# Hybrid decoder step on one core: chunk 0 cast from raw x with the norm's weight as scale, matmuls of ones ahead, and the work ahead of chunk 2 put in another order

## The chip, the cores and the metric

One NeuronCore of a Trainium2 chip runs the whole step. The time is device time in microseconds, the median of several runs; the three runs of the kernel before gave 1186.17, 1187.00 and 1188.01 us. Engines are called as in the profile: PE is TensorE, DVE is VectorE, ACT is ScalarE, POOL is GpSimd, SP the queue that issues the DMAs.

## The reference

One layer on 2048 prompt tokens and 64 tokens of eight running sequences, 1024 wide:

```python
xn = rms_norm(x, norm_pre)                  # x * rsqrt(mean(x*x) + eps) * norm_pre
z  = xn @ w_in                              # 1024 -> 4096: v_pool, g_pool, u_lru, g_lru
y_pool = (windowed mean of v_pool - v_pool) @ pool_w * pool_scale     # windows 2, 4, 8, 16
xs = causal_conv(u_lru)                     # width 4
y_lru = scan(a(xs), u(xs))                  # gates: sigmoid(xs @ wa + ba), sigmoid(xs @ wx + bx)
out = concat(y_pool * silu(g_pool), y_lru * silu(g_lru)) @ w_out
y = x + rms_norm(out, norm_post)
```

Everything is float32. The kernel writes each operand of a large product as a rounded high part and a low part, and adds three products (high x high, high x low, low x high).

## The kernel before, in words

The 2112 tokens are cut into five chunks of 426 (the last has 408). `x` comes twice: transposed (`xt`, model channels on partitions, the moving operand of the products) and by token (`x`, 17 tiles of 128 tokens, called tok 0 to 16), from which the norm's factor r of each token is made.

How r is made: `tok_square` squares a token tile on ACT and sums it; `tok_rsqrt(i0, i1)` makes rsqrt for a range of tiles (DVE, two ACT steps, three DVE steps); `r_diag(c)` multiplies the identity by the factors of the tiles of chunk c (ACT, four or five pieces); `r_rows(c)` multiplies ones by that diagonal on PE, so that r of chunk c stands on all partitions in PSUM. The text calls these results r0 to r4. `normalise(c, r)` multiplies `xt` by r and the norm's weight (DVE, L272), casts the high part (ACT, L280) and subtracts for the low part (DVE or POOL, L289); it squares some token tiles between its casts.

Chunk 0 doesn't wait for its r: its x is multiplied by the norm's weight alone (`x_g` on DVE, `x_hi` on ACT, `x_lo` on DVE or POOL), and r0 is multiplied in after the product (`pool_evac` with `rs`, and L719 for the gates).

The first part of the program, up to L723, loads all this and does the blocks of pool group 0 for chunk 0: value blocks 0 and 1 (`v0_0`, `v1_0`) and gate blocks (`g0_0`, `g1_0`), each 8 steps of 3 matmuls (`z_k`). The loop at L728 does chunks 1 to 4 of the same group. For chunk 1 it does both value blocks, r2, one gate block, the pool map of chunk 0 (`pool_mm`, 12 matmuls) and the other gate block; normalising of chunk 2 goes on meanwhile. In chunk 2 comes value block 0, then r3, then value block 1. A pool map needs the windows of its chunk (`pool_window`, DVE L365 to L391, then a cast and a low part).

The order of work on each engine is the order of the code (the block stands under `tc.manual_schedule()`), and each engine takes its instructions one after the other. Loads go through the one SP queue in the order of the code; a load into a slot waits until the tile in it has been squared, and holds the loads behind it. Three slots hold three token tiles each; the slot of a tile is chosen by its number.

Of the kernel before, what the change touches and what calls it, by code (L numbers as in the profile page):

```python
# [55 lines left out]
R01_AT = 3  # L56
# [5 lines left out]
def hymba_kernel(  # L62
# [196 lines left out]
    def normalise(c, r, lo_engs, squares={}):  # L259
# [10 lines left out]
        for k in range(KT):  # L270
# [347 lines left out]
    with tc.manual_schedule():  # L618
        nc.sync.dma_start(out=parT, in_=par)
        load_x(0, 0, 1)  # L620
        stage_w(0, 0, 1)
        load_x(0, 1, 2)
        load_x(0, 2, 4)
        stage_w(1, 0, 1)
# [27 lines left out]
        x_g(2)
        x_hi(2)
        x_g(3)
        x_hi(3)
        x_lo(2, V)
        w_hi(0, 1, A)
        x_lo(3, G)
        w_lo(0, 1, V)
        x_g(4)  # L660
        x_hi(4)
        x_g(5)
        x_hi(5)
        x_lo(4, V)
        x_g(6)
        x_hi(6)
        x_lo(5, G)
# [2 lines left out]
        x_g(7)  # L670
        x_hi(7)
        x_lo(6, V)
        x_lo(7, V)
# [3 lines left out]
        for i in range(3):  # L677
# [811 lines left out]
```

## Time and profile before

| | |
|---|---|
| median of three runs | 1187.0 us (1186.17 to 1188.01) |
| the profiled execution | 1190.4 us, of which the span from first to last instruction 1188.4 us |
| PE busy | 1167.1 us, 98% |
| DVE, ACT, POOL busy | 828.8 us (70%), 552.4 us (46%), 356.9 us (30%) |
| granted TensorE clock, mean | 0.997 |

Times in the rows are from the span's start. A matmul's row starts when it starts; its length holds the way out of the array, so that the distance of two starts, not the length, is what one costs. In a row of the timeline the brackets at the end give the idle time of that engine just before it, and what ended it.

### The profile page before, as it was taken

What the parts mean: (1) busy time and instruction counts of PE and PEld (TensorE: products, weight loads), DVE (VectorE), ACT (ScalarE), POOL (GpSimd) and SP (SyncE); (2) the same over time, 40 slices, a digit from 0 to 9 for tenths busy, and PEclk for the clock granted to TensorE, in tenths of its full rate; (3) what the DMA queues carried; (4) which work ended last, traced back from release to release, by engine and by line L of the source; (5) the groups of instructions that cost most, each with busy time, mean ns of one, the idle gap of its engine ahead of it and who ended that gap; (6) DMA issues with size and microseconds to landing.
All of it is one profiled execution on the core that took longest, in us unless ns stands there. A gap on an engine that the chain in (4) does not pass through costs nothing.

```text
span 1188.4 us, 16263 instructions
## 1 busy us (share of the span) xinstructions
PE 1167.1 (98%) x5794; PEld 1076.0 (91%) x5794; DVE 828.8 (70%) x1201; ACT 552.4 (46%) x1015; POOL 356.9 (30%) x486
## 2 busy tenths in 40 slices
PE   7999999999999999999999999999999999999997
PEld 6899999999999999999999999999878878888886
DVE  4787334443625557888888888889877668888787
ACT  5753311211231236767676776767745233345232
POOL 4145402410431243333333433334310002221332
PEclk9999999999999999999999999999999999999999
DMA  9712533532630210111111111104479766767553
GB/s 344 264 59 65 188 132 111 183 115 79 199 94 30 67 49 26 45 44 40 38 40 53 49 45 45 40 34 120 134 217 286 212 188 202 220 204 231 151 168 133
DMA packets 127905, 146.94 MB, mean 124 GB/s; under 512 B 12432, under 2 KB 87440, under 8 KB 127824
## 3 DMA queue, kind: packets, MB, share of 16 engines
q1 hardware_dynamic: 127824, 145.91, 39.3%
q8 instruction: 45, 0.74, 0.3%
q14 instruction: 36, 0.29, 0.1%
HBM read 106.37 MB, written 39.24 MB: 123 GB/s over the span
## 4 chain that ended last, share of the span: by engine, by line
PE 84%; DVE 5%; DMA 5%; ACT 3%; issue 2%; POOL 1%; SPq 0%; DVEq 0%; ACTq 0%; POOLq 0%
PE p L979 7%; PE p L978 7%; PE p L977 7%; PE v L302 5%; PE v L304 5%; PE v L303 5%; PE u L302 5%; PE u L304 5%; PE u L303 5%; PE g L302 5%; PE lg L302 5%; PE lg L304 5%; PE lg L303 5%; PE g L303 5%; PE g L304 5%
## 5 line engine op out<-in xcount | busy, mean ns | idle before, releaser
L504 DVE SCALAR_TENSOR_TENSOR xs<-u,parT,xs 128x426 f32<-128x426 f32 (+1 forms) x120 | 109.2, 910 | 46.7 <-ACT xs L500 30.5
L302 PE MATMUL v<-xh,w 128*128 128x426 f32 (+2 forms) x320 | 116.9, 365 | 7.1 <-ACT w L595 6.0
L303 PE MATMUL v<-xl,w 128*128 128x426 f32 (+2 forms) x320 | 116.1, 363 | 0.9 <-DVE xl L611 0.6
L970 POOL TENSOR_TENSOR xr<-ac,xr 128x512 f32<-128x512 f32 x28 | 47.7, 1723 | 229.7 <-DVE ac L1108 125.5
L302 PE MATMUL g<-xh,w 128*128 128x426 f32 (+1 forms) x320 | 114.6, 358 | 0.0
L304 PE MATMUL v<-xh,w 128*128 128x426 f32 (+2 forms) x320 | 114.1, 362 | 0.4 <-DVE w L109 0.4
L304 PE MATMUL g<-xh,w 128*128 128x426 f32 (+1 forms) x320 | 113.9, 356 | 0.2 <-POOL w L109 0.2
L303 PE MATMUL g<-xl,w 128*128 128x426 f32 (+1 forms) x320 | 113.8, 356 | 0.0
L302 PE MATMUL u<-xh,w 128*128 128x426 f32 (+1 forms) x320 | 113.7, 355 | 0.0
L302 PE MATMUL lg<-xh,w 128*128 128x426 f32 (+1 forms) x320 | 113.7, 355 | 0.0
L304 PE MATMUL lg<-xh,w 128*128 128x426 f32 (+1 forms) x320 | 113.5, 355 | 0.0
L304 PE MATMUL u<-xh,w 128*128 128x426 f32 (+1 forms) x320 | 113.4, 354 | 0.0
L303 PE MATMUL lg<-xl,w 128*128 128x426 f32 (+1 forms) x320 | 113.4, 354 | 0.0
L303 PE MATMUL u<-xl,w 128*128 128x426 f32 (+1 forms) x320 | 113.3, 354 | 0.0
L1270 DVE RECIPROCAL rv<-rv 128x426 f32<-128x426 f32 (+1 forms) x40 | 112.4, 2811 | 0.0
L977 PE MATMUL p<-ws,s 128*128 128x512 f32 (+1 forms) x264 | 102.4, 388 | 0.0
L978 PE MATMUL p<-ws,s 128*128 128x512 f32 (+1 forms) x264 | 102.0, 386 | 0.2 <-DVE ws L109 0.2
L979 PE MATMUL p<-ws,s 128*128 128x512 f32 (+1 forms) x264 | 102.0, 386 | 0.1
L979 PE MATMUL p<-ws,a 128*128 128x512 f32 x192 | 75.8, 395 | 1.1 <-DVE a L109 1.1
L978 PE MATMUL p<-ws,a 128*128 128x512 f32 x192 | 75.8, 395 | 1.1 <-DVE ws L109 1.1
L977 PE MATMUL p<-ws,a 128*128 128x512 f32 x192 | 75.8, 395 | 0.3 <-ACT ws L106 0.3
L365 DVE TENSOR_TENSOR s<-e 128x440 f32<-128x440 f32 (+3 forms) x40 | 28.8, 720 | 64.2 <-ACT e L336 48.5
(225 smaller groups left out, 2805.5 us busy)
## 6 DMA issues: line engine op xcount, KB each, us to landing
a<-mixed SPq DMA_DIRECT2D x112, 256.0 KB, 4.3
wr<-in_w_in SPq DMA_DIRECT2D x56, 256.0 KB, 3.1
tok<-in_x SPq DMA_DIRECT2D x16, 512.0 KB, 10.2
wo<-in_w_out SPq DMA_DIRECT2D x32, 256.0 KB, 3.8
wtd<-wo SPq DMA_DIRECT2D x32, 256.0 KB, 2.4
w<-wtd SPq DMA_DIRECT2D x32, 256.0 KB, 3.8
xr<-in_x SPq DMA_DIRECT2D x32, 256.0 KB, 3.8
out<-xr SPq DMA_DIRECT2D x30, 256.0 KB, 2.6
```

The lines of the kernel that those rows point to most:

```text
L302: nc.tensor.matmul(out, lhsT=wh, rhs=xh, start=(k == 0), stop=False)
L303: nc.tensor.matmul(out, lhsT=wh, rhs=xl, start=False, stop=False)
L304: nc.tensor.matmul(out, lhsT=wl, rhs=xh, start=False, stop=(k == KT - 1))
L365: nc.vector.tensor_tensor(out=dst[:, first:L], in0=src[:, first:L], in1=src[:, first - sh:L - sh], op=ALU.add)
L504: nc.vector.scalar_tensor_tensor(out=xs, in0=E[:, k:k + n], scalar=col(C_CW + 8 * k, b), in1=xs, op0=ALU.mult, op1=ALU.add)
L970: (eng or nc.vector).tensor_tensor(out=out, in0=a, in1=b, op=op)
L977: nc.tensor.matmul(out, lhsT=ah, rhs=wh, start=start and k == 0, stop=False)
L978: nc.tensor.matmul(out, lhsT=ah, rhs=wl, start=False, stop=False)
L979: nc.tensor.matmul(out, lhsT=al, rhs=wh, start=False, stop=stop and k == KT - 1)
L1270: nc.vector.reciprocal(out=v, in_=v)
```

## The change

It touches the part ahead of chunk 2 alone.

- Chunk 0: `x_g` goes. ACT casts the high part from raw x with the norm's weight as scale, and DVE makes every low part from raw x, the weight and the high part in one instruction. DVE casts the weights' high parts of both value blocks.
- PE: eight matmuls of a 128x128 tile of ones with itself ahead of the first value matmul, and two more behind each of the first three steps. Value block 1 runs two steps behind block 0 instead of four.
- Loads: the parameters come third; tok 3 to 6, which chunk 1's r needs, ahead of tok 0 to 2; tok 9 ahead of chunk 3's x; chunk 1's x in four pieces.
- r1 alone is made in gate block 1 of chunk 0, two steps later than before; r0 moves into chunk 1's first gate block, and with it the evictions of chunk 0 (`first_evac`) and squares 8 and 9; r2 moves into chunk 1's second gate block. Both gate blocks now stand ahead of chunk 0's pool map.
- Squares: tok 0, 1, 2, 7 between the casts of chunk 1; 10, 11, 12 between those of chunk 2, each followed by the load of tok 13, 14, 15 into its slot; 13 to 16 behind them.

```diff
-R01_AT = 3
+R1_AT = 5
+R0_AT = 2
+R2_AT = 4
+N_WARM = 8
+N_FILL = 2
@@ normalise
                 nc.scalar.copy(out=xn[c][0][:, p], in_=src)
+                lo()
+                los.append((p, src))
                 for j in squares.get(k, ()):
                     tok_square(j)
-                lo()
-                los.append((p, src))
+                    if j in reload:
+                        load_tok(reload[j], slots[2], j % 3)
...
     def x_hi(k):
-        A.copy(out=xn[0][0][:, k * CW:(k + 1) * CW], in_=xg[k])
-
-    def x_lo(k, eng):
+        A.activation(out=xn[0][0][:, k * CW:(k + 1) * CW], in_=x_part(0, k), func=AF.Copy, scale=col(C_NP, k))
+
+    def x_lo(k):
         p = slice(k * CW, (k + 1) * CW)
-        eng.tensor_tensor(out=xn[0][1][:, p], in0=xg[k], in1=xn[0][0][:, p].bitcast(F32), op=ALU.subtract)
+        V.scalar_tensor_tensor(out=xn[0][1][:, p], in0=x_part(0, k), scalar=col(C_NP, k),
+                               in1=xn[0][0][:, p].bitcast(F32), op0=ALU.mult, op1=ALU.subtract)
...
-        nc.sync.dma_start(out=parT, in_=par)
         load_x(0, 0, 1)
         stage_w(0, 0, 1)
+        nc.sync.dma_start(out=parT, in_=par)
...
-        for i in range(3):
-            load_tok(i, slots[0])
+        for i in range(3, 7):
+            load_tok(i, slots[i // 6 * 2], i % 3)
         for h in range(2):
             nc.sync.dma_start(out=w9r[h], in_=w_in[9, :, 512 * h:512 * (h + 1)])
...
+        for k in range(0, KT, 2):
+            load_x(1, k, k + 2)
+        for i in range(3):
+            load_tok(i, slots[1], i)
+        for i in range(7, 9):
+            load_tok(i, slots[2], i % 3)
...
+        warm = s_psum("warm")[:, :P]
+
+        def ones_mm(n):
+            for _ in range(n):
+                nc.tensor.matmul(warm, lhsT=ones, rhs=ones, start=True, stop=True)
+
+        ones_mm(N_WARM)
...
-        lag = 4
+        lag = 2
         for k in range(KT + lag):
             if k < KT:
                 z_k(Z0[0], wt[0], 0, k)
+            if k < lag + 1:
+                ones_mm(N_FILL)
             if k >= lag:
                 z_k(Z0[1], wt[1], 0, k - lag)
...
         r_diag(1)
-        r_diag(0)
-        for k in range(KT):
-            if k == R01_AT:
-                r1, R0 = r_rows(1), r_rows(0)
-                A.copy(out=r0, in_=R0)
-            z_k(Z0[3], wt[9], 0, k)
-        normalise(1, r1, [V], {3: (7,), 5: (8,), 7: (9,)})
...
+        for k in range(KT):
+            if k == R1_AT:
+                r1 = r_rows(1)
+            z_k(Z0[3], wt[9], 0, k)
+        normalise(1, r1, [V], {1: (0,), 3: (1,), 5: (2,), 7: (7,)})
+        tok_rsqrt(0, 3)
+        r_diag(0)
         pw0 = split_small(pw0r, 512, "pw0")
...
+        def first_evac():
+            R0 = r_rows(0)
+            A.copy(out=r0, in_=R0)
+            for j in range(2):
+                E, prevE0[j] = pool_evac(j, j, 0, Z0[j], None, r0)
+                Es.append(E)
+            for j in range(2):
+                V.tensor_tensor(out=sgs0[j], in0=Z0[2 + j], in1=r0, op=ALU.mult)
...
             if c == 1:
                 for k in range(KT):
                     for j in range(2):
                         z_k(Z[j], wt[j], c, k)
-                r = r_rows(n)
+                Zg = [gate(0, R0_AT, first_evac, s_psum)]
                 for j in range(2):
                     evac(j)
-                Zg = [gate(0)]
+                for i in range(8, 10):
+                    tok_square(i)
+                tok_rsqrt(7, 10)
+                r_diag(2)
+                for i in range(10, 13):
+                    load_tok(i, slots[2], i % 3)
+                for j in range(2):
+                    ds0.append(pool_window(j, 0, 0, Es[j]))
+                r2 = []
+                Zg.append(gate(1, R2_AT, lambda: r2.append(r_rows(2))))
+                r = r2[0]
...
             if c == 1:
-                for i in range(15, 17):
-                    load_tok(i, slots[2])
+                for i in range(13, 17):
                     tok_square(i)
+                    if i == 13:
+                        load_tok(16, slots[2], 1)
                 tok_rsqrt(10, 17)
                 r_diag(3)
                 silus()
```

How the order moves. PE, gate block 1 of chunk 0 before: `r_305` is r1 and `r_310` is r0, `g_0_115` the gate block.

```order
L304 MATMUL g_0_115<-xh_106,w_0_104 128x426
L255 MATMUL r_305<-dg_286,ones 128x86
L255 MATMUL r_305<-dg_286,ones 128x128 x2
L255 MATMUL r_305<-dg_286,ones 128x84
L255 MATMUL r_310<-dg_291,ones 128x128 x3
L255 MATMUL r_310<-dg_291,ones 128x42
L302 MATMUL g_0_115<-xh_106,w_0_104 128x426
```

PE in chunk 1's first gate block (`g_1_406`) of the kernel after: `r_413` is r0.

```order
L308 MATMUL g_1_406<-xh_316,w_0_102 128x426
L309 MATMUL g_1_406<-xl_317,w_0_102 128x426
L310 MATMUL g_1_406<-xh_316,w_0_102 128x426
L259 MATMUL r_413<-dg_346,ones 128x128 x3
L259 MATMUL r_413<-dg_346,ones 128x42
```

r0 has moved behind the whole of chunk 1's value blocks.

ACT from the copy of r0 to the diagonal of r2 (`dg_370`) before; the squares are the rows that write `tok` from `tok`.

```order
L703 COPY r_111<-r_310 128x426
L280 CAST xh_331<-xr_136 128x426 x2
L280 CAST xh_331<-xr_136 128x852
L224 ACTIVATE tok_110,tok<-tok_110 128x1024
...
L224 ACTIVATE tok_109,tok<-tok_109 128x1024
L230 ACTIVATE tok<-tok 128x3
L231 ACTIVATE tok<-tok 128x3
L248 ACTIVATE dg_370<-ident,tok 128x44
```

The same stretch after, where `dg_468` is the diagonal of r2 and `e_1` are the evictions of chunk 1's value blocks.

```order
L706 COPY r_111<-r_413 128x426
L342 COPY e_1_450<-v_1_356 128x426
L342 COPY e_1_455<-v_1_357 128x426
L228 ACTIVATE tok_110,tok<-tok_110 128x1024 x2
L234 ACTIVATE tok<-tok 128x3
L235 ACTIVATE tok<-tok 128x3
L252 ACTIVATE dg_468<-ident,tok 128x44
```

The copy of r0 stood ahead of the casts of chunk 1; it now stands behind them, and squares 8 and 9 stand behind it.

ACT from the third square inside chunk 2's casts to the diagonal of r3 before (`dg_545`):

```order
L224 ACTIVATE tok_110,tok<-tok_110 128x1024
L280 CAST xh_514<-xr_144 128x852
L224 ACTIVATE tok_110,tok<-tok_110 128x1024
L224 ACTIVATE tok_110,tok<-tok_110 64x1024
L230 ACTIVATE tok<-tok 128x7
L231 ACTIVATE tok<-tok 128x7
L248 ACTIVATE dg_545<-ident,tok 128x2
```

and after (`dg_578`):

```order
L228 ACTIVATE tok_110,tok<-tok_110 128x1024
L284 CAST xh_543<-xr_148 128x852
L228 ACTIVATE tok_110,tok<-tok_110 128x1024 x3
L228 ACTIVATE tok_110,tok<-tok_110 64x1024
L234 ACTIVATE tok<-tok 128x7
L235 ACTIVATE tok<-tok 128x7
L252 ACTIVATE dg_578<-ident,tok 128x2
```

Two squares stood between the last cast and the rsqrt; now four do.

## Rows read from the trace of the kernel before

**Rows 1.** The page's first part: busy time of each engine, share of the span, instructions.

```profile
PE 1167.1 (98%) x5794; PEld 1076.0 (91%) x5794; DVE 828.8 (70%) x1201; ACT 552.4 (46%) x1015; POOL 356.9 (30%) x486
```

**Rows 2.** Busy time by stage: the stage, its length, busy time of PE, PEld, DVE, ACT and POOL with instructions, granted TensorE clock, DMA share and GB/s.

```profile
0.00:60.50 60.50, 51.32 (x228) 45.81 (x229) 36.33 (x67) 40.97 (x81) 17.90 (x41) 0.97 0.81 299
60.50:140.00 79.50, 79.50 (x440) 77.68 (x440) 49.84 (x98) 32.62 (x64) 36.77 (x41) 1.00 0.30 93
```

**Rows 3.** Timeline of PE, chunk 0: start, length, engine, line, operation, tiles, form, count, idle time before and what ended it.

```profile
5.99 0.72 PE L302 MATMUL v<-xh,w 128*128 128x426 f32 x1 [5.99 <-ACT w L595]
...
11.18 0.72 PE L303 MATMUL v<-xl,w 128*128 128x426 f32 x1 [0.58 <-DVE xl L611]
...
13.75 0.72 PE L302 MATMUL v<-xh,w 128*128 128x426 f32 x1 [0.40 <-ACT xh L607]
...
19.52 0.40 PE L302 MATMUL v<-xh,w 128*128 128x426 f32 x1
...
23.65 0.36 PE L302 MATMUL g<-xh,w 128*128 128x426 f32 x1
```

**Rows 4.** Timeline of PE around r1 with r0 (30.06), the end of chunk 1's value blocks (44.06), r2 (45.60), the start of chunk 2 (60.53) and r3 (65.20).

```profile
30.06 1.87 PE L255 MATMUL r<-dg,ones 128*128 128x86 f32 x16
31.76 0.44 PE L302 MATMUL g<-xh,w 128*128 128x426 f32 x1
...
44.06 0.35 PE L304 MATMUL v<-xh,w 128*128 128x426 f32 x1
45.60 0.42 PE L255 MATMUL r<-dg,ones 128*128 128x44 f32 x2 [1.19 <-ACT dg L248]
46.40 1.38 PE L255 MATMUL r<-dg,ones 128*128 128x128 f32 x6 [0.38 <-ACT dg L248]
...
60.53 0.36 PE L302 MATMUL v<-xh,w 128*128 128x426 f32 x1
...
65.20 1.20 PE L255 MATMUL r<-dg,ones 128*128 128x2 f32 x10
66.24 0.44 PE L302 MATMUL v<-xh,w 128*128 128x426 f32 x1
```

**Rows 5.** Busy time of the stretch behind r2's wait, columns as in rows 2.

```profile
46.90:50.30 3.40, 3.40 (x12) 3.24 (x12) 2.92 (x10) 3.40 (x8) 0.71 (x1) 0.50 0.16 63
```

**Rows 6.** Timeline of ACT in chunk 2's normalising: the third square (tok 14), the last square's accumulator read (tok 16), and four pieces of r3's diagonal.

```profile
55.94 1.06 ACT L224 ACTIVATE tok<-tok 128x1024 f32<-128x1024 f32 x1
...
60.03 0.19 ACT L224 ACTIVATION_READ_ACCUMULATOR tok<-tok 64x1 f32 x1
...
61.54 1.21 ACT L248 ACTIVATE dg<-ident,tok 128x128 f32<-128x128 f32 x4 [0.45 <-DVE tok L234]
```

**Rows 7.** DMA issues in five narrow stretches: tiles, queue, operation, count, KB each, us from issue to landing. In order: issued at 1.72, at 5.35 (the last piece of chunk 0's x), at 26.98 (tok 9), at 53.34 (tok 15) and at 55.19 (tok 16).

```profile
wst<-in_w_in SPq DMA_DIRECT2D x1, 256.0 KB, 3.2
...
xr<-in_xt SPq DMA_DIRECT2D x1, 426.0 KB, 6.8
...
tok<-in_x SPq DMA_DIRECT2D x1, 512.0 KB, 16.5
...
tok<-in_x SPq DMA_DIRECT2D x1, 512.0 KB, 3.7
...
tok<-in_x SPq DMA_DIRECT2D x1, 256.0 KB, 3.6
```

**Rows 8.** Timelines of DVE and POOL in chunk 0: low part of the first weight, the last two low parts of x on DVE, and what POOL did then.

```profile
5.97 0.69 DVE L598 TENSOR_TENSOR w<-wst,w 128x512 fp32r<-128x512 f32 x1
...
16.01 3.28 DVE L611 TENSOR_TENSOR xl<-x0g,xh 128x426 fp32r<-128x426 f32 x2
...
15.81 4.64 POOL L598 TENSOR_TENSOR w<-wst,w 128x512 fp32r<-128x512 f32 x3 [0.65 <-DVE w L595]
```

**Rows 9.** Timeline of ACT: diagonals of r1 and r0, copy of r0, accumulator read of tok 9's square and the last three pieces of r2's diagonal, evictions of chunk 1's value blocks.

```profile
28.69 2.31 ACT L248 ACTIVATE dg<-ident,tok 128x86 f32<-128x86 f32 x8 [0.70 <-DVE tok L234]
...
31.97 0.52 ACT L703 COPY r<-r 128x426 f32<-128x426 f32 x1 [0.97 <-PE r L255]
...
43.49 1.06 ACT L224 ACTIVATE tok<-tok 128x1024 f32<-128x1024 f32 x1 [3.27 <-DMA tok<-in_x]
44.46 0.19 ACT L224 ACTIVATION_READ_ACCUMULATOR tok<-tok 128x1 f32 x1
...
45.94 0.98 ACT L248 ACTIVATE dg<-ident,tok 128x128 f32<-128x128 f32 x3 [0.40 <-DVE tok L234]
...
50.32 0.91 ACT L336 COPY e<-v 128x426 f32<-128x426 f32 x2
```

**Rows 10.** Timeline of DVE, normalising of chunk 1: first products, first and last low part.

```profile
31.12 1.23 DVE L272 SCALAR_TENSOR_TENSOR xr<-xr,parT,r 128x426 f32<-128x426 f32 x2 [2.52 <-PE r L255]
32.97 0.61 DVE L289 TENSOR_TENSOR xl<-xr,xh 128x426 fp32r<-128x426 f32 x1 [0.62 <-ACT xh L280]
...
40.26 1.04 DVE L289 TENSOR_TENSOR xl<-xr,xh 128x852 fp32r<-128x852 f32 x1 [0.80 <-ACT xh L280]
```

**Rows 11.** Timeline of DVE: last step of the rsqrt for r2, first step of chunk 0's windows, first products and last two low parts of chunk 2.

```profile
45.75 0.16 DVE L234 SCALAR_TENSOR_TENSOR tok<-tok 128x3 f32<-128x3 f32 x1
...
46.84 0.59 DVE L365 TENSOR_TENSOR s<-e 128x426 f32<-128x426 f32 x1
...
50.10 2.37 DVE L272 SCALAR_TENSOR_TENSOR xr<-xr,parT,r 128x426 f32<-128x426 f32 x4 [0.34 <-issue]
...
57.11 2.10 DVE L289 TENSOR_TENSOR xl<-xr,xh 128x852 fp32r<-128x852 f32 x2
```

More of the change, by code (lines that the diff above doesn't have):

```diff
@@ L215, in hymba_kernel, with load_tok @@
     tok_box = {}
-    def load_tok(i, slot):
+    def load_tok(i, slot, pos):
         lo, hi = i * P, min((i + 1) * P, T_ALL)
-        t = tok_box[i] = slot[:hi - lo, i % 3 * D:(i % 3 + 1) * D]
+        t = tok_box[i] = slot[:hi - lo, pos * D:(pos + 1) * D]
         nc.sync.dma_start(out=t, in_=x[lo:hi, :])
@@ L257, in r_rows, with normalise @@
         return R
-    def normalise(c, r, lo_engs, squares={}):
+    def normalise(c, r, lo_engs, squares={}, reload={}):
         W = XR[c][1] - XR[c][0]
@@ L618, in hymba_kernel @@
     with tc.manual_schedule():
-        nc.sync.dma_start(out=parT, in_=par)
         load_x(0, 0, 1)
         stage_w(0, 0, 1)
+        nc.sync.dma_start(out=parT, in_=par)
         load_x(0, 1, 2)
+        stage_w(1, 0, 1)
         load_x(0, 2, 4)
-        stage_w(1, 0, 1)
         stage_w(0, 1, 2)
@@ L641, in hymba_kernel @@
         load_x(2, 0, 8)
-        x_g(0)
+        warm = s_psum("warm")[:, :P]
[3 more added lines that the diff above has]
+        ones_mm(N_WARM)
         x_hi(0)
-        w_hi(0, 0, A)
-        x_lo(0, V)
+        w_hi(0, 0, V)
+        x_lo(0)
         w_lo(0, 0, V)
-        x_g(1)
         x_hi(1)
-        x_lo(1, G)
+        x_lo(1)
         w_hi(1, 0, V)
         w_lo(1, 0, G)
[L652 to L658, printed above, removed]
-        w_lo(0, 1, V)
[L660 to L667, printed above, removed]
+        for k in range(2, 4):
+            x_hi(k)
+            x_lo(k)
+        w_hi(0, 1, V)
+        w_lo(0, 1, V)
+        for k in range(4, 6):
+            x_hi(k)
+            x_lo(k)
         w_hi(1, 1, V)
         w_lo(1, 1, G)
[L670 to L673, printed above, removed]
+        for k in range(6, 8):
+            x_hi(k)
+            x_lo(k)
         for h in range(2):
@@ L676, in hymba_kernel @@
             w_lo(8, h, G)
-        for i in range(3):
+        for i in range(3, 7):
             tok_square(i)
@@ L681, in hymba_kernel @@
             w_lo(9, h, G)
-        for i in range(3, 7):
-            tok_square(i)
-        for i in range(7, 9):
-            load_tok(i, slots[2])
+        load_tok(9, slots[2], 0)
         load_x(3, 0, KT)
-        lag = 4
+        lag = 2
         for k in range(KT + lag):
@@ L690, in hymba_kernel @@
                 z_k(Z0[0], wt[0], 0, k)
+            if k < lag + 1:
+                ones_mm(N_FILL)
             if k >= lag:
                 z_k(Z0[1], wt[1], 0, k - lag)
-        for i in range(9, 12):
-            load_tok(i, slots[1])
-        tok_rsqrt(0, 7)
+        tok_rsqrt(3, 7)
         for k in range(KT):
@@ L735, in evac, with gate @@
                 E[j], prev[j] = pool_evac(j, j, c, Z[j], prev[j], None)
-            def gate(j):
-                Zg = z_psum(f"g{j}_{c}")[:, :W]
+            def gate(j, at=None, then=None, ps_tile=z_psum):
+                Zg = ps_tile(f"g{j}_{c}")[:, :W]
                 for k in range(KT):
+                    if k == at:
+                        then()
                     z_k(Zg, wt[8 + j], c, k)
@@ L771, in hymba_kernel @@
             if n:
-                last = normalise(n, r, LO_ENGS[n], {1: (12,), 3: (13,), 5: (14,)} if c == 1 else {})
+                last = normalise(n, r, LO_ENGS[n], {1: (10,), 3: (11,), 5: (12,)} if c == 1 else {},
+                                 {i: i + 3 for i in range(10, 13)})
             if c == 1:
-                for i in range(15, 17):
-                    load_tok(i, slots[2])
+                for i in range(13, 17):
                     tok_square(i)
+                    if i == 13:
+                        load_tok(16, slots[2], 1)
                 tok_rsqrt(10, 17)
@@ L786, in hymba_kernel @@
                 hr = [fold_load(1, 0)]
-            Zg.append(gate(1))
+            if c > 1:
+                Zg.append(gate(1))
             todo_silu = Zg
```

26 lines of the change are left out of this document (1 added, 25 removed).

## The prediction, made before the changed kernel was run

> **What bounds the kernel now.** I read the page first, then the busy time by stage, then the timelines of the first 66 us. TensorE is busy 98% of the span [rows 1]. The stages show where the rest lies: of the first 60.5 us it works 51.3, and from 60.5 to 140 it works all 79.5 at full clock [rows 2]. So a microsecond gained or lost ahead of chunk 2 is carried to the end, and the change touches that part alone. TensorE's long waits there are two: 5.99 us for the first operands [rows 3], and 1.19 + 0.38 us for the scales of chunk 2, r2 [rows 4].
>
> The timeline shows one more loss. Value matmuls of 426 columns stand about 0.355 us apart until 19.52 and 0.195 us after it, though the engine waits no more from 13.75 on [rows 3]; 426 columns at 1.2 GHz are 0.355 us. The profile's clock column does not show that phase, the spacing does. The wait for r2 is followed by the same thing: after those 1.57 us the granted clock is 0.50 for 3.4 us [rows 5], which costs 1.7 us.
>
> The place that decides is r3, the scales of chunk 3: a few small matmuls that TensorE reaches at 65.20 [rows 4]. ScalarE has finished their operand at 61.54 + 1.21 = 62.75 [rows 6]. That chain (squares of the token tiles, rsqrt, diagonal) is only 2.45 us ahead of TensorE. If TensorE comes earlier and the chain does not, the gain ends there.
>
> **The change, step by step.** The sum follows both chains from the start to r3; times are from the span's start.
>
> *Start.* The parameters are now the third issue. The piece issued in that place, at 1.72, took 3.2 us [rows 7]: 4.9. The cast (0.55 us) no longer waits for a VectorE product: first value matmul about 5.5 instead of 5.99. A cast that scales by a column has no row of this size; bounds are the plain 0.55 and some 0.2 more, as the diagonals (128 columns, 0.32 apart, with such a scale) cost about that above a plain cast [rows 9]. I take 0.55; only the first of the eight is on the path. The new low part, one instruction of two inputs, is like the products of chunk 1, 0.6 us [rows 10], what the subtraction alone took.
>
> *Clock and value blocks.* After its last start wait at about 6.8 (VectorE makes the low parts of x and of the weight one after the other, 0.6 and 0.7 us [rows 8]) the filler keeps TensorE going. Before, 5.8 us without a wait went ahead of the fast spacing (13.75 to 19.52); I take the same: 12.6. One ones matmul is 128 of the 852 fp32 columns that took 1.70 us (30.06 to 31.76 [rows 4]), 0.26 us at full and 0.5 at half clock, so the six fillers take 3.0 us of the 7.1 between 5.5 and 12.6, waits 1.0, and about 9 of 48 matmuls the rest. 39 x 0.195 = 7.6: the value blocks end at 20.2, not 23.65 [rows 3]. Supply does not hold them: the last x lands at 5.35 + 6.8 = 12.15 [rows 7], its casts end about 13.2, and two low parts at the 1.6 us each that VectorE showed beside GpSimd [rows 8] give 16.5. Moving the low parts from GpSimd to VectorE costs nothing while that is so; should the clock be fast from the start, they are the bound (rival 1).
>
> *r1.* 39 more matmuls (gate block 0, five steps of gate block 1), 7.6 us: 27.8 (30.06 before). Its diagonal started at 28.69 behind seven squares [rows 9]; four are left, three of 1.04 us less, and its four pieces take 1.2: 26.8 at the latest. No wait. r1 is half of the 1.70 us: 28.65; VectorE starts at 28.85.
>
> *Chunk 1 normalised.* Before: 31.12 to 41.3, 10.2 us, with waits of 0.62 us behind the copy of r0 and 0.80 behind a late token tile [rows 10]. Both go: 8.8, end 37.65. TensorE reaches chunk 1 at 30.4, only 9 matmuls behind r1 where it had 15, and now waits for the low parts: about 0.3, 0.4 and 1.0 us (ready 1.85, 3.5 and 5.7 us after VectorE's start, wanted at 30.4, 32.0 and 33.5). 48 matmuls and 1.7: end 41.5, before 44.26 [rows 4].
>
> *r0 and r2.* Tile 9, now issued ahead of chunk 3's x about 24 us (once tile 6 is squared), has landed by 41 even at its old 16.5 us [rows 7], and square 9 wants it at 46. Two steps (1.2) and r0 (0.85): 43.5. ScalarE's queue now holds, behind that: copy of r0 0.5, two evictions 0.9, squares 8 and 9 at 1.06 [rows 9]: 47.2. From a square's end to the last piece of a diagonal it was 44.65 to 46.92, 2.3 [rows 9]: 49.5. TensorE does 30 matmuls and is there at 49.3. So the r2 stall goes, 1.57 us and 1.7 of clock. r2, 12 matmuls, the pool map's 12: chunk 2 could start at 55.0, where it was 60.53 [rows 4]. TensorE has gained 5.5 us here.
>
> *VectorE and ScalarE have not.* VectorE's rsqrt ends 1.25 after the square (44.65 to 45.9 [rows 11]): 48.45. The windows of chunk 0, until now done while TensorE was elsewhere, come here: 2.9 us (46.84 to 50.10 less 0.34 idle). Chunk 2's normalising starts at 51.3, before 50.10 [rows 11]: 1.2 us later. It takes 9.1 (to 59.2), so to 60.4, and TensorE, which eats a step of one block in 0.6 us, is held by it and reaches r3 at 61.0, 4.2 earlier than before.
>
> *Squares.* Before, tiles 12, 13, 14 were squared inside this stage and 15, 16 behind it. Now it is 10, 11, 12, and four are left. The reloads of 13, 14 and 15 wait for the slots of 10, 11 and 12. The third square of the stage ended 6.95 us after its start (55.94 + 1.06 [rows 6] against 50.10): 58.3. Then tile 15 is loaded into that slot, 3.7 us on an idle queue [rows 7]: 62.0. Squares 15 and 16, 2.3: 64.3 (16's own load, 3.6 us [rows 7], started earlier, behind square 13). On SP the reloads hold back only the stores of chunk 0's pool map, which come after r3. From the end of the last square to the last piece of the diagonal it was 60.2 to 62.75, 2.55 [rows 6]: 66.9, before 62.75. So 4.15 later, against a slack of 2.45.
>
> On the load the Trainium skill, DMA: Bandwidth & Descriptors, section "Anatomy of one DMA", gives 2.0 us fixed and the bytes at 436 GB/s for another path: 3.2 us for 512 KB, by my estimate. By it the sum below would be 0.5 smaller; the row's 3.7 decides.
>
> *At r3.* TensorE idles from 61.0 to about 65.2 (first, 2-column piece) and 0.8 more; r3 ends 0.3 behind the last piece, 67.2 against 66.24: +1.0. 5 us of idleness is three times what went ahead of the halved clock at r2, so I add that price once, +1.7; bounds are 0 (it stays) and 3.4 (two such stretches). What follows is bound by TensorE as before.
>
> Sum: +1.0 + 1.7 = +2.7 us. The profiled execution took 1190.4 with a span of 1188.4; it would be 1193.1. The median of the runs is 1187.0, 3.4 below it; +2.7 on that is **1189.7 us**.
>
> **Rivals.**
> 1. *The clock is free sooner.* If the ones matmuls alone bring the fast spacing before the first value matmul, the value blocks are bound by the low parts: 16.5, less what is then done, about 17.9 instead of 20.2. All steps up to the diagonal of r3 follow from r1, so 2.3 us come off: +1.0 - 2.3 + 1.7 = +0.4, 1187.4. For it: the ones are there from the start, so the eight can run through the 5 us in which TensorE idled. Against it: no row shows what matmuls of constants do to the clock, and those of 11 to 13.7 us, with gaps of 0.4 to 0.6 us between them, did not raise it [rows 3]. The Trainium skill, TensorE: Matmul & The Clock Gate, Part 1, "What's actually happening", says that the low clock is the resting state, that activity releases it, and that the moment is not tied to a kernel's start; by it this rival would come true in some executions and not in others.
> 2. *The 1187.0 holds no r2 stall.* The profiled execution is 3.4 us above the median, and its r2 stall is 1.57 + 1.7 = 3.3 us; tile 9 landed 16.5 us after its issue [rows 7], in a full queue. If it lands sooner in unprofiled runs, there is nothing left to save at r2, and the chain to r3, which no full queue holds, stays where it is: +2.7 + 3.3 = +6.0, 1193.0. Against it: some of the 3.4 may be the profiler's.
> 3. *The r3 wait does not come* (not slower). If reloads and squares hide so that the diagonal is there at 62.75 as before, TensorE waits 1.7 us instead of 5: r3 ends at 63.1, -3.1, and with the clock kept 1183.9. It decides from a diagonal at about 63.5 on. For it: ScalarE is idle between squares while reloads are under way. Against it: each load, square and rsqrt in the chain has a row, and their order is fixed.
>
> **How the numbers follow.** Forecast (r3 wait of 4 to 5 us, clock price once) 0.42, on its own 1188.0 to 1191.4; rival 1 0.26; rival 2 0.18; rival 3 0.14. A change below 0.2% (2.4 us) can't be told from none. Slower: rival 2 and about three quarters of the forecast, 0.50. Same: the rest of the forecast and rival 1, 0.37. Faster: rival 3, 0.13. The range goes from inside rival 3 and the lower half of rival 1 (1186.2) to rival 2 (1193.2).
>
> **What would show it.** First value matmul 5.3 to 5.7; fast spacing from about 12.6 (before 8: rival 1); r1 near 28; r2 without a wait; chunk 2's first matmul near 55; then TensorE waiting 4 to 5 us for ScalarE's diagonal at r3, with four squares behind chunk 2's last cast, and a clock of 0.50 behind it. No r3 wait, or a diagonal before 63.5, would make the forecast wrong, and so would a place later than chunk 2 that gives back or takes more than 1 us.

## The result, and the profile after

The changed kernel took 1191.65 us, the median of 7 runs (1190.91 to 1195.05), beside 1188.01 for the kernel before on the same chip; the ratio is 1.0038, 95% interval 1.0026 to 1.0051. On 1187.5 us, about the median of the kernel before in the later comparisons, the ratio is +4.5 us (3.1 to 6.1). The ratio is formed from all runs; the two medians alone differ by 3.6 us. The forecast was +2.7 us, below that interval.

The profiled execution took 1190.91 us with a span of 1189.0. The page's first part answers to [rows 1]; TensorE is as busy as before.

```profile
PE 1168.5 (98%) x5822; PEld 1079.1 (91%) x5822; DVE 829.3 (70%) x1202; ACT 552.9 (47%) x1015; POOL 355.0 (30%) x483
```

The busy time by stage, columns as in [rows 2]: the first 60.5 us, then two short stretches in which the granted clock is 0.50 (level 1.2 GHz), then up to 140.

```profile
0.00:60.50 60.50, 54.18 (x270) 49.40 (x270) 33.90 (x66) 36.95 (x73) 14.39 (x38) 0.97 0.78 282
12.20:15.60 3.40, 3.40 (x11) 3.19 (x10) 3.40 (x6) 2.74 (x5) 1.43 (x1) 0.50 1.03 420
...
66.80:73.60 6.80, 5.58 (x19) 5.30 (x20) 4.14 (x10) 5.71 (x15) 1.41 (x2) 0.50 0.12 44
73.60:140.00 66.40, 66.40 (x362) 64.87 (x362) 45.50 (x87) 25.56 (x48) 34.83 (x39) 1.00 0.29 84
```

Of the first 60.5 us TensorE is now busy 54.18 (51.32 in [rows 2]), the ones matmuls included. From 66.8 to 73.6 it works 5.58 of 6.8 us, and at half clock. The timeline of TensorE says why; it answers to [rows 3] and [rows 4]: the ones matmuls, the first value matmul, the wait for step 2, gate block 0 (21.08), r1, r0, r2, the start of chunk 2 (56.51), r3 in two parts and the second value block (70.34).

```profile
1.12 3.79 PE L648 MATMUL warm<-ones 128*128 128x128 f32 x16 [1.12 <-DVE ones L122]
5.67 0.46 PE L308 MATMUL v<-xh,w 128*128 128x426 f32 x1 [0.77 <-ACT xh L607]
...
10.33 0.46 PE L308 MATMUL v<-xh,w 128*128 128x426 f32 x1 [1.42 <-ACT xh L607]
...
21.08 0.35 PE L308 MATMUL g<-xh,w 128*128 128x426 f32 x1
...
28.63 1.01 PE L259 MATMUL r<-dg,ones 128*128 128x86 f32 x8
...
43.50 0.98 PE L259 MATMUL r<-dg,ones 128*128 128x128 f32 x8
...
50.23 1.05 PE L259 MATMUL r<-dg,ones 128*128 128x44 f32 x8
...
56.51 0.35 PE L308 MATMUL v<-xh,w 128*128 128x426 f32 x1
...
67.76 0.59 PE L259 MATMUL r<-dg,ones 128*128 128x2 f32 x2 [4.80 <-ACT dg L252]
68.61 1.93 PE L259 MATMUL r<-dg,ones 128*128 128x128 f32 x8 [0.27 <-ACT dg L252]
70.34 0.70 PE L308 MATMUL v<-xh,w 128*128 128x426 f32 x1
```

r1, r0 and r2 wait for nothing (their rows have no brackets). Chunk 2 starts 4.0 us sooner than in [rows 4]. Then TensorE stands still for 4.80 + 0.27 us at r3, and the second value block, at 66.24 before, starts at 70.34.

What r3 waits for is on ScalarE: the squares of tiles 13 to 16 behind the casts of chunk 2, and the diagonal.

```profile
60.49 1.06 ACT L228 ACTIVATE tok<-tok 128x1024 f32<-128x1024 f32 x1
...
62.34 1.06 ACT L228 ACTIVATE tok<-tok 128x1024 f32<-128x1024 f32 x1 [0.70 <-DMA tok<-in_x]
...
63.66 1.06 ACT L228 ACTIVATE tok<-tok 128x1024 f32<-128x1024 f32 x1 [0.17 <-DMA tok<-in_x]
...
65.69 1.06 ACT L228 ACTIVATE tok<-tok 64x1024 f32<-64x1024 f32 x1 [0.88 <-DMA tok<-in_x]
...
68.16 1.21 ACT L252 ACTIVATE dg<-ident,tok 128x128 f32<-128x128 f32 x4 [0.45 <-DVE tok L238]
```

Three of the four wait for their reload. The last, tile 16, is issued behind square 13 (60.49 + about 1.0); the list of DMA issues between 61 and 62 gives it 3.9 us, so it lands near 65.4, and its square starts at 65.69:

```profile
tok<-in_x SPq DMA_DIRECT2D x1, 256.0 KB, 3.9
```

### The profile page after: what moved, and what is told of

It reads as the page before. It is cut to its first block, busy times and chain, and to the rows that moved or that the text cites. A ratio compares the mean times of both kernels' runs of the same rounds, so it can differ in the third digit from the quotient of the medians.

```text
span 1189.0 us, 16330 instructions
## 1 busy us (share of the span) xinstructions
PE 1168.5 (98%) x5822; PEld 1079.1 (91%) x5822; DVE 829.3 (70%) x1202; ACT 552.9 (47%) x1015; POOL 355.0 (30%) x483
## 4 chain that ended last, share of the span: by engine, by line
PE 79%; DMA 7%; DVE 7%; ACT 4%; issue 2%; POOL 1%; SPq 0%; DVEq 0%; ACTq 0%; POOLq 0%
PE p L983 6%; PE p L984 6%; PE p L982 6%; PE v L309 5%; PE v L308 5%; PE v L310 5%; PE u L308 5%; PE u L310 5%; PE u L309 5%; PE lg L308 5%; PE lg L310 5%; PE lg L309 5%; PE g L308 4%; PE g L310 4%; PE g L309 4%; DMA a<-mixed 3%
```

## Experiments

All compare with the kernel before on the same chip. "us off" is the ratio less one, times 1187.5. Theory 1 is the forecast's (the wait for r3's diagonal and the clock behind it), theory 2 that waits further on take up what is gained or lost ahead, theory 3 that the loss is elsewhere.

**e1: squares and reloads sooner.**

```diff
         pw0 = split_small(pw0r, 512, "pw0")
+        for i in range(8, 10):
+            tok_square(i)
+            load_tok(i + 3, slots[2], i % 3)
...
-                for i in range(8, 10):
-                    tok_square(i)
                 tok_rsqrt(7, 10)
                 r_diag(2)
                 for i in range(10, 13):
-                    load_tok(i, slots[2], i % 3)
+                    tok_square(i)
+                    load_tok(i + 3, slots[2], i % 3)
```

> Edit: squares 8 and 9 go ahead of r0's copy on ScalarE (idle there for 3.04 us), squares 10 to 13 behind r2's diagonal and between the windows, each reload behind the square that frees its place, and the rsqrt of r3 works on tiles 10 to 13 alone, inside chunk 2's normalising. Theory 1 (the loss is the wait for r3's diagonal): the diagonal is done by about 60, TensorE reaches r3 at 62.5 to 64 and waits less than 0.5 us, the clock stays full, and the second value block of chunk 2 starts at 63.5 to 65 (70.34 in the changed kernel, 66.24 in the one before). If that is carried to the end, 7 us come off: 1184 to 1185. Theory 2 (waits behind chunk 2, 0.58 us near 144 and 1.65 us near 245 in the kernel before, take back what comes early): the same profile up to 140, but larger waits there, and 1186 to 1188. Theory 3 (the loss is not at r3): 1190 to 1192.

Measured 1185.81 us, ratio 0.9989 (0.9978 to 0.9999): -1.3 us off, and so 5 to 6 us less than the changed kernel. The r3 wait is gone (timeline of TensorE: two waits of the pool map of chunk 0, then r3 and the second value block):

```profile
53.92 0.46 PE L332 MATMUL y<-dh,pw 128*128 128x426 f32 x1 [0.68 <-ACT dh L110]
55.16 0.46 PE L333 MATMUL y<-dl,pw 128*128 128x426 f32 x1 [0.78 <-POOL dl L113]
...
63.39 1.20 PE L267 MATMUL r<-dg,ones 128*128 128x2 f32 x10
64.42 0.44 PE L318 MATMUL v<-xh,w 128*128 128x426 f32 x1
```

64.42 is where theory 1 put it; the total lies between theories 1 and 2, since 7 us were to come off and 5 to 6 did. Theory 3 falls. The edit moves squares and cuts r3's rsqrt at once, so it does not tell the two apart; e2 does. The squares that I moved now stand in front of the pool map's casts: 0.39, 0.68 and 0.78 us of waits, and 3.4 us at half clock behind them.

**e2: only r3's rsqrt cut.** In both kernels one rsqrt serves tiles 10 to 16, but the tokens of chunk 3 end in tile 13: r3 needs no square of 14 to 16.

```diff
-                for i in range(13, 17):
-                    tok_square(i)
-                    if i == 13:
-                        load_tok(16, slots[2], 1)
-                tok_rsqrt(10, 17)
+                tok_square(13)
+                load_tok(16, slots[2], 1)
+                tok_rsqrt(10, 14)
                 r_diag(3)
+                for i in range(14, 17):
+                    tok_square(i)
+                tok_rsqrt(14, 17)
```

> Edit: in the changed kernel only the rsqrt of r3 is cut: tiles 10 to 13, then r3's diagonal, then squares 14 to 16 and their rsqrt. Theory 1: square 13 ends at 63.5, the diagonal at about 66, so r3's wait falls from 5.1 to 2 us or less and the second value block of chunk 2 starts 3.5 to 4.5 us sooner, at 66 to 67. But VectorE has the windows of chunk 1 behind the rsqrt of tiles 14 to 16, which ends at 69 or later, and TensorE needs them for chunk 1's pool map behind that block, so a wait of 2 to 3 us comes there: 1189 to 1191 in all. Theory 3 (the loss is not at r3): no wait moves, 1190 to 1192; a gain of over 4 us would say that nothing else hangs on these squares.

Measured 1188.5 us, ratio 1.0013 (1.0002 to 1.0024): +1.5 us, some 2 to 3 us less than the changed kernel. The timeline of TensorE shows r3's wait at 0.32 us, the second value block, and the next wait where it was expected:

```profile
61.57 1.22 PE L259 MATMUL r<-dg,ones 128*128 128x128 f32 x8 [0.32 <-ACT dg L252]
62.62 0.44 PE L308 MATMUL v<-xh,w 128*128 128x426 f32 x1
...
69.83 0.43 PE L322 MATMUL y<-dh,pw 128*128 128x426 f32 x1 [2.31 <-ACT dh L110]
```

The second value block comes sooner than the 66 to 67 expected: in this execution the whole start is 1.8 us sooner (gate block 0 at 19.24 beside 21.08), and square 13 was expected too late. The second profile of the changed kernel (e12) has as early a start, 19.36, and yet waits 5.18 us at r3 and reaches that block at 68.98. Behind the wait of 2.31 us the clock is halved from 71.75 to 75.16.

So the squares of tiles 14 to 16 with their rsqrt end two chains: r3's diagonal in the changed kernel, and the windows of chunk 1, which VectorE has behind that rsqrt. Here none of these squares waits for its reload; they stand behind r3's diagonal on ScalarE. The last one, in ScalarE's timeline:

```profile
64.31 1.05 ACT L228 ACTIVATE tok<-tok 64x1024 f32<-64x1024 f32 x1
```

**e3: the kernel before with a late r3.**

```diff
                 tok_rsqrt(10, 17)
+                for _ in range(7):
+                    A.copy(out=tok_box[14], in_=tok_box[14])
                 r_diag(3)
```

> Edit: in the kernel before, seven copies of one token tile onto itself (128x1024, about 1.0 us each) stand on ScalarE ahead of r3's diagonal, which then ends near 70. Nothing else changes. Theory 1: TensorE waits about 4.5 us at r3, the clock halves behind it for one or two stretches of 3.4 us, and at the end of chunk 2's value blocks the kernel is 5 to 7 us late. If that is carried to the end: 1193 to 1195. Theory 2 (the waits near 144 and 245 take up 2.2 us or more of a delay): 1190.5 to 1192.5. Theory 3 (a wait at r3 costs nothing much): 1188 to 1189.

Measured 1196.08 us, ratio 1.0073 (1.0059 to 1.0087): +8.7 us (7.0 to 10.3), more than any theory gave. In its profile TensorE waits 4.28 us at r3; the second fence is the busy time behind it.

```profile
68.43 2.13 PE L255 MATMUL r<-dg,ones 128*128 128x2 f32 x10 [4.28 <-ACT dg L248]
...
75.97 0.36 PE L316 MATMUL y<-dh,pw 128*128 128x426 f32 x1
```

```profile
68.90:72.20 3.30, 3.30 (x13) 3.21 (x14) 0.83 (x2) 3.27 (x8) 0.00 (x0) 0.50 0.00 0
```

r3's ten matmuls took 2.13 us where they took 1.20 [rows 4]: from 68.84 they ran at half clock too. A wait of this length, put into a kernel without any of the change, makes TensorE as late at the pool map of chunk 1 as the change does (75.97 beside 75.57 to 76.57 below). Theory 2 falls: against e9 the profile is 6.4 us late there and 7.1 at the end, so nothing was taken up.

In time it costs more than the change, 8.7 us beside 3.7 to 4.9, and the intervals do not overlap. Why stays open; the seven copies also put off all that stands behind them on ScalarE, so e3 is not a late r3 alone.

**e4: the kernel before with tile 9 loaded sooner.**

```diff
+        load_tok(9, slots[1])
         load_x(3, 0, KT)
...
-        for i in range(9, 12):
+        for i in range(10, 12):
             load_tok(i, slots[1])
```

> Edit: in the kernel before, the load of token tile 9 is issued ahead of chunk 3's x. The stall for r2 (1.57 us and 1.7 us of halved clock) should be gone. Forecast's step: chunk 2 starts 3.3 us sooner, near 57.2, then r3 waits about 0.9 us for its diagonal (62.75), so 2.4 us are left at the second value block (63.8 against 66.24); 1185.5 if carried, 1187 to 1188 if the waits near 144 and 245 take it. Rival 2 (timed runs hold no r2 stall): 1187 to 1188 as well, but then e1 must not be faster than the kernel before either, and e3 must cost its full 5 us.

Measured 1184.97 us, ratio 0.9984 (0.9975 to 0.9992): -1.9 us. r2 waits for nothing at 44.50, and r3, at 62.13, did not wait either: with r2 sooner ScalarE and VectorE are sooner as well, which my 0.9 us left out. One load's place gives the r2 gain without the price at r3.

**e5: e1 without its new waits.** The windows stand between the squares, r3's rsqrt one step later.

```diff
                 for i in range(10, 13):
                     tok_square(i)
                     load_tok(i + 3, slots[2], i % 3)
+                    if i < 12:
+                        ds0.append(pool_window(i - 10, 0, 0, Es[i - 10]))
```

> Edit: as e1, but the windows of chunk 0 stand between squares 10 to 12 instead of behind them, and square 13 and the rsqrt of r3 go one step later into chunk 2's normalising, so that neither chunk 0's pool map (waits of 0.39, 0.68 and 0.78 us in e1) nor VectorE (2.54 us in e1) waits for a square. Theory 1: no wait at the pool map and none at r3, no halved stretch near 56, the second value block of chunk 2 starts at 60.5 to 61.5 instead of 64.4, and 3 to 4 us come off e1's 1185.8: 1182 to 1183, so a microsecond gained ahead of chunk 2 is carried to the end. Theory 2 (something later takes it): 1185 to 1186 as in e1.

Measured 1185.18 us (1180.89 to 1190.16, 12 runs), ratio 0.9979 (0.9966 to 0.9992): -2.5 us, and no clear gain over e1. The pool map waits no more and chunk 2 starts at 53.63, but VectorE's low parts do not follow: TensorE waits 0.62 and 1.42 us for them, and in the profile the clock halves at 60.04. A miss: the second value block started at 63.95, not 61, half a microsecond ahead of e1's. The time is the one that theory 2 gave, but with so little gained ahead of the pool map, e5 decides nothing between the two.

**e6: e5 with more ones matmuls.**

```diff
-N_WARM = 8
-N_FILL = 2
+N_WARM = 11
+N_FILL = (2, 8, 2)
```

> Edit: as e5, with 11 instead of 8 ones matmuls ahead and 2, 8 and 2 instead of 2, 2 and 2 between the first value steps, so that TensorE has work in the waits of 1.43 us (before the first value matmul) and 1.42 us (for the high part of step 2). If those waits are what lowered the granted clock at 8 to 12 us, it stays full from the first matmuls on, gate block 0 starts near 19.5 to 20 instead of 21.08, and all behind it comes 1 to 1.5 us sooner: 1181 to 1182. If the clock falls for another reason, or the low parts hold TensorE, it equals e5 or is up to 1 us longer.

Measured 1183.96 us, ratio 0.9968 (0.9953 to 0.9982): -3.8 us, between its two expectations; the interval overlaps e5's. The timeline of TensorE at the start, and the busy time up to 60:

```profile
8.94 1.95 PE L658 MATMUL warm<-ones 128*128 128x128 f32 x16
...
19.31 0.35 PE L318 MATMUL g<-xh,w 128*128 128x426 f32 x1
```

```profile
6.40:60.00 53.60, 50.43 (x271) 46.77 (x271) 34.81 (x66) 39.51 (x84) 12.91 (x17) 1.00 0.86 316
```

The clock stays at 1.00 where the changed kernel lost it at 12.18, which speaks for the waits as the reason, and gate block 0 starts 1.8 us sooner than there. But in e5's execution the clock held without the added matmuls, and gate block 0 came at 18.94: they are not needed for it, and whether they make a full clock likelier is not shown by the two profiles that have them (e6 and e10).

**e7: the changed kernel without ones matmuls** (`N_WARM` and `N_FILL` 0).

> Edit: the changed kernel without any matmul of ones. Forecast's step: TensorE starts the value matmuls at 0.355 us spacing and goes over to 0.195 near 12.5 to 13; gate block 0 then starts at 21 to 22 (21.08 in the changed kernel), and since the chain to r3 follows r1, all of it moves by the same 0 to 1 us: 1191 to 1193. Rival (the ones matmuls are what makes the start fast): gate block 0 at 23 or later and 1193.5 to 1195.

Measured 1192.52 us, ratio 1.0041 (1.0027 to 1.0055): +4.9 us, not to be told from the +4.5 with them. The fast spacing began later than the 12.5 to 13 expected, gate block 0 a little sooner than the 21 to 22. The timeline of TensorE: first value matmul, the first one at 0.195 us spacing, and gate block 0.

```profile
5.61 0.72 PE L308 MATMUL v<-xh,w 128*128 128x426 f32 x1 [5.61 <-ACT xh L607]
...
15.17 0.36 PE L308 MATMUL v<-xh,w 128*128 128x426 f32 x1
...
20.43 0.35 PE L308 MATMUL g<-xh,w 128*128 128x426 f32 x1
```

**e8: the kernel before with ones matmuls** (8 ahead, 2 in each of the first three steps).

> Edit: the kernel before, with the eight ones matmuls ahead and two in each of the first three value steps. TensorE gets through the value blocks 1 to 3 us sooner (gate block 0 at 20.5 to 22.5, 23.65 before), but r1 needs a diagonal that ScalarE finishes near 29.9 behind seven squares, so the gain turns into a wait of 1 to 2.5 us at r1, chunk 1 starts where it did, and the time is that of the kernel before, 1186.5 to 1188.5, or 1 to 2 us more where the wait halves the clock. If instead it is 1184 to 1185, r1 was not a bound in the kernel before.

Measured 1185.13 us, ratio 0.9982 (0.9972 to 0.9993): -2.1 us, a miss. Gate block 0 came at 22.94, a little later than expected; the wait at r1 came as expected, and r2's was short:

```profile
30.68 2.35 PE L255 MATMUL r<-dg,ones 128*128 128x86 f32 x16 [1.17 <-ACT dg L248]
...
45.68 0.42 PE L255 MATMUL r<-dg,ones 128*128 128x44 f32 x2 [0.21 <-ACT dg L248]
46.48 1.07 PE L255 MATMUL r<-dg,ones 128*128 128x128 f32 x6 [0.38 <-ACT dg L248]
```

In this profile TensorE comes to the pool map of chunk 1 no sooner than in e9 below. Where the 2 us come from stays open.

**e9: the kernel before, a second profile.**

> The kernel before, unchanged, for a second profile: which of the stalls of the first profile belong to the kernel and which to that one execution. If the waits near 144 (0.58 us), 245 (1.65 us) and 961 to 967 (1.3 us) belong to the kernel, they are here again, and what TensorE gains or loses ahead of them is partly taken up there. If they belong to the execution, most are missing and the span is 2 to 4 us shorter than 1188.4. The stall for r2 (1.19 and 0.38 us) should be here again by the forecast; by rival 2 it is not. Its halved stretch is missing in the profile of e3, which has the same program up to there.

One run, 1186.78 us with a span of 1184.8, 3.6 us less than the first profile. The timeline of TensorE at r2, r3 and the pool map of chunk 1:

```profile
45.28 0.42 PE L255 MATMUL r<-dg,ones 128*128 128x44 f32 x2 [0.83 <-ACT dg L248]
46.08 1.07 PE L255 MATMUL r<-dg,ones 128*128 128x128 f32 x6 [0.38 <-ACT dg L248]
...
63.82 1.20 PE L255 MATMUL r<-dg,ones 128*128 128x2 f32 x10
...
69.60 0.36 PE L316 MATMUL y<-dh,pw 128*128 128x426 f32 x1
```

r2's stall is here again (0.83 + 0.38 us), so rival 2 falls, but no halved clock follows it. The waits near 144 and 245 are 0 and 0.30 us, those between 959 and 964 are 1.5 (1.3 in the first profile, 0.3 in the changed kernel). The first two belong to the execution, not to the kernel. The late ones are in both profiles of this kernel, but the two of the changed kernel differ there too (0.3, and 1.2 in e12), so they come and go as well.

**e10: e6 with r2's rsqrt ahead of chunk 0's evictions.**

```diff
             load_tok(i + 3, slots[2], i % 3)
+        tok_rsqrt(7, 10)
...
-                tok_rsqrt(7, 10)
                 r_diag(2)
```

> Edit: as e6, with the rsqrt of r2 right behind square 9, ahead of the evictions of chunk 0, where VectorE has nothing to do. The windows of chunk 0 and so chunk 2's normalising start about 1.2 us sooner, and TensorE's waits for chunk 2's low parts (0.61 and 1.25 us in e6) shrink to under 0.8 us together. If a microsecond ahead of r3 is carried to the end: about 1 us off e6, 1182 to 1183.5. If something else holds it: as e6, 1184.

Measured 1181.96 us, ratio 0.9959 (0.9943 to 0.9975): -4.9 us (3.0 to 6.8), the lowest median here, below both kernels; its interval overlaps e6's. TensorE has one wait left in chunk 2:

```profile
57.72 0.47 PE L319 MATMUL v<-xl,w 128*128 128x426 f32 x1 [0.97 <-DVE xl L305]
60.06 1.20 PE L267 MATMUL r<-dg,ones 128*128 128x2 f32 x10
61.09 0.44 PE L318 MATMUL v<-xh,w 128*128 128x426 f32 x1
```

**e11: e4 and e8 together.**

> Edit: e4 and e8 together in the kernel before: tile 9 loaded ahead of chunk 3's x, and the ones matmuls. Each alone gave about 2 us. If e8 gained because r2 was waited for less often or with less loss of clock, the two take the same loss away and do not add: 1184.5 to 1185.5. If e8's gain was at the start, they add: 1182.5 to 1183.5.

Measured 1183.98 us, ratio 0.9973 (0.9962 to 0.9983): -3.2 us, between the two expectations.

**e12: the changed kernel, a second profile.**

> The changed kernel, unchanged, for a second profile and more times. Against the second profile of the kernel before (e9) the first one is 7.0 us late behind chunk 2's value blocks, but 4.2 us at the end, since e9 holds 1.8 us of stalls between 957 and 970 and this one 0.3. If those late stalls are chance, and what is lost at r3 is carried, this execution has some of them again and the timed difference is 4.5 to 6.5 us. If the changed kernel takes something back by itself at a later place, the late stalls are missing again and it is 3.5 to 4.5 us. The wait at r3 is 4.5 to 5.5 us with two halved stretches in either case; without the filled first waits the clock at 8 to 15 us may come out otherwise.

Measured 1191.05 us (11 runs), ratio 1.0031 (1.0015 to 1.0047): +3.7 us (1.8 to 5.6). The profiled run was the longest, 1195.17 us. r3 waits as before, and 6.8 us at half clock follow:

```profile
66.40 0.59 PE L259 MATMUL r<-dg,ones 128*128 128x2 f32 x2 [5.18 <-ACT dg L252]
67.25 1.93 PE L259 MATMUL r<-dg,ones 128*128 128x128 f32 x8 [0.27 <-ACT dg L252]
68.98 0.70 PE L308 MATMUL v<-xh,w 128*128 128x426 f32 x1
```

It also has stalls of 1.72 us near 249 and 1.19 us near 971, which the first one lacks: chance in this kernel as well.

**All runs together.** The pool map of chunk 1 is the first place behind chunk 2's value blocks. Its start in each kernel's profile, less e9's 69.60, beside the timed difference:

| kernel | pool map of chunk 1 | less 69.60 | timed, us off |
|---|---|---|---|
| e10 | 65.83 | -3.8 | -4.9 |
| e6 | 66.94 | -2.7 | -3.8 |
| e11 | 67.45 | -2.2 | -3.2 |
| e4 | 67.91 | -1.7 | -1.9 |
| e5 | 68.70 | -0.9 | -2.5 |
| e1 | 69.16 | -0.4 | -1.3 |
| e2 | 69.83 | +0.2 | +1.5 |
| e8 | 70.01 | +0.4 | -2.1 |
| e12 (changed) | 75.57 | +6.0 | +3.7 |
| e3 | 75.97 | +6.4 | +8.7 |
| e7 | 76.00 | +6.4 | +4.9 |
| changed | 76.57 | +7.0 | +4.5 |

The first profile of the kernel before, at 70.99, is not in the table. A straight line through the twelve has a slope of 0.99 and passes 0.9 us below zero. Single profiles scatter by up to 3.3 us about it (e3; e2 is 2.2 above it, since its wait of 2.31 us has halved clock behind it). On the whole, what TensorE gains or loses up to there is carried to the end one for one.

The timelines say it more directly. The first matmul that writes `p`, in e9 and in the changed kernel:

```profile
844.68 0.39 PE L977 MATMUL p<-ws,a 128*128 128x512 f32 x1
...
851.11 0.39 PE L982 MATMUL p<-ws,a 128*128 128x512 f32 x1
```

The changed kernel is 6.4 us late there, e7 6.3, e3 6.9, and e12, which lost more near 249, 9.4: what r3 cost is not taken up in the 770 us behind it. At the end of the spans they are 4.2, 6.0, 7.1 and 8.4 us behind e9.

## Why the prediction was right, point by point

The sign, the place and the mechanism were right; the sum was too small by 1 to 2 us, +2.7 for +3.7 and +4.5. The 1191.65 us lie inside the stated range (1186.2 to 1193.2) and just above the forecast's own part of it (1188.0 to 1191.4).

That it came so near is in part luck. At the pool map of chunk 1 the changed kernel is 5.6 us later than the first profile of the kernel before (76.57 against 70.99), where the sum had 2.7; the diagonal and the clock make up the rest, as below. The profiled execution, forecast at 1193.1, took 1190.91, since the first profile of the kernel before loses 2.4 us in stalls near 144 and 245 that the changed kernel's does not have, and some 2 us more behind 845.

- *Start* (5.5): 5.67. The scaled cast takes 0.65 us, inside the bounds of 0.55 and 0.75, and the new low part 0.66, the subtraction 0.6.
- *Clock and value blocks* (end at 20.2): 21.08, on another course. Rival 1's condition came true, and its gain did not: the granted clock was full from 5.35 (the trace's record of it begins there; the sixteen passes of the ones ahead took 3.79 us, in e6 at full clock 1.95), fell to 0.50 at 12.18 behind the wait of 1.42 us for step 2, and came back at 15.59. Without ones matmuls (e7) the fast spacing began at 15.17 and gate block 0 at 20.43. The eight ones matmuls and the six fillers thus gave nothing in this kernel. The Trainium skill, TensorE: Matmul & The Clock Gate, Part 1, "What's actually happening", says that the moment of release is not tied to a kernel's start. The traces agree: with the same eight ones in front, the clock was full from 5.35 in the changed kernel, from 4.80 in its second profile (e12), from 10.31 in e2 and from 12.75 in e8.
- *r1* (27.8), *chunk 1 normalised* (8.8 us), *r0* (done at 43.5): 28.63, 8.75 us (29.69 to 38.44), 43.50 to 44.31, no waits at r1 and r0. Value blocks end at 42.35 (41.5).
- *r0 and r2* (no stall at r2, 49.3; chunk 2 at 55.0): no stall, 50.23; 56.51, with 0.46 us at the pool map for GpSimd that I had not counted. What this is worth was overrated: the 1.7 us of halved clock in [rows 5] is missing in e9 and e3, so two of three profiles put the stall at 1.2 to 1.5 us, not 3.3, and e4, which removes it alone, gained 1.9.
- *VectorE and ScalarE have not* (normalising of chunk 2 from 51.3; r3 reached at 61.0): 52.89 and 62.9. The windows took 3.8 us instead of 2.9. One row explains 0.9 of it: an operation on a single column took 1.07 us (0.15 in its twin), while GpSimd worked on a low part from 51.29 to 52.75. The Trainium skill, SBUF — State Buffer, "Terms", says that the two engines share a pair of ports which one holds alone for a whole instruction; the row agrees, it ends 0.02 us behind GpSimd's. The timelines of VectorE and GpSimd:

```profile
50.28 0.15 DVE L396 TENSOR_TENSOR df<-s,rcnt 128x1 f32<-128x1 f32 x1
...
51.70 1.07 DVE L396 TENSOR_TENSOR df<-s,rcnt 128x1 f32<-128x1 f32 x1
52.80 0.16 DVE L397 TENSOR_TENSOR d<-df,e 128x1 f32<-128x1 f32 x1
52.89 2.36 DVE L276 SCALAR_TENSOR_TENSOR xr<-xr,parT,r 128x426 f32<-128x426 f32 x4
...
51.29 1.46 POOL L113 TENSOR_TENSOR dl<-d,dh 128x426 fp32r<-128x426 f32 x1 [4.31 <-ACT dh L110]
```

- *Squares* (last square 64.3, diagonal 66.9): 66.8 and 69.4. This is the term that was mis-sized, by 2.5 us. 1.4 us come from the later start (the third square of the stage ended at 59.7, not 58.3; its 6.95 is 6.90 by the rows); the rest is that I let tile 15's load be the last. Tile 16's, which I put off as "started earlier", waits for square 13, and that stands behind the last cast of chunk 2. And e2 shows that r3 had to wait for none of tiles 14 to 16, had their rsqrt been a step of its own; the sum took the one rsqrt for given.
- *At r3* (wait 4.2 + 0.8; r3 ends at 67.2): 4.80 + 0.27, and the next block at 70.34. TensorE was 1.9 us later than forecast and the diagonal 2.5, so the wait came out right by luck, two errors of nearly the same size, and its end did not. r3's matmuls themselves ran at half clock, 2.6 us with the short wait in them instead of 1.0.
- *The clock price* (1.7, bounds 0 and 3.4): 6.8 us at half, two stretches as in the upper bound. TensorE worked 5.58 of them, so they cost about 2.8 us. Against e9, r3 reached 0.9 us sooner, waits of 5.1, 1.3 more in r3's matmuls and 1.5 behind them make the +7.0 at the pool map of chunk 1.

Rival 2 was wrong in its mechanism (the stall is there in e9), though right that the first profile makes too much of it. The 3.4 us between the first profile and the median were mostly neither r2 nor the profiler: e9 is 3.6 us shorter, 1.4 of it ahead of the pool map of chunk 1 and 2.2 in stalls behind. Rival 3 did not come; e1 and e10 show what it would have taken, squares and reloads moved along with the change. The forecast named as a sign of being wrong a place later than chunk 2 that gives back or takes more than 1 us. In single executions there are such places: behind 845 us the changed kernel's first profile gains 2.3 us on e9, and e12 loses 3 near 249. They do not go with the kernel: behind 845 e7 gains 0.3 and e12 1.0. That 7.0 us in the profile are 4.5 timed lies within the scatter of the table, but all three profiles with the late r3 of the change lie below its line, and why the timed loss is smaller than the lateness at the pool map stays open.

## What to carry to other kernels

When an edit lets the bound engine run ahead, follow every chain that feeds it for the next few stages, with each reload behind the use that frees its place: here 4 us gained at chunk 2 turned into 5 us of waiting at r3, since four squares, three of them waiting for a load, stood ahead of its diagonal. Squares moved ahead (two of them into an idle gap of ScalarE), with r3's rsqrt cut, took the kernel from +4 to -1 us, three more steps (e5, e6, e10) to -5. Cut a step that serves many tiles where its first reader needs only some: in e2 that alone gave 2 to 3 us. Price a long wait of TensorE as the wait plus the half clock inside and behind it, and take a second profile of the baseline before a stall of 1 to 2 us goes into a sum.

## What the runs showed of the hardware

Matmuls of constants alone brought the granted clock to 1.00 at 4.5 to 6.4 us (where the trace's record of it begins) in seven of the nine profiles that have them, before any real matmul or with the first; in e2 and e8 it came at 10.31 and 12.75. Waits of 1.2 to 1.4 us in that phase were followed by a halved clock in the changed kernel, e1 and e12, waits of 0.9 and 0.8 us in e11 too, one of 0.9 us in e5 not; in e6 and e10, where ones matmuls fill them, it stayed full. The wait of 1.2 to 1.6 us for r2 halved it in one of three profiles of the same code. Waits of 4.3 to 5.2 us at r3 halved it in all four, for 3.4 us once and for 6.8 us three times, and in those three from before TensorE went on. Elsewhere it halved behind waits of 1.42 us in e5 and 2.31 in e2, and not behind 1.25 in e6, 1.17 in e8 and 0.97 in e10. So a wait of 1 to 2 us has no one price here.
